# Row tiles 6, 4 and half of 5 loaded ahead of the last weight slices, and the third row tile of each later triple loaded first, in a matmul-tanh-multiply kernel

## The chip, the cores and the metric

The kernel runs on one core of a Trainium2 chip. The metric is the device time of one execution in microseconds: the median of the runs, beside the one execution that the hardware profiler took apart. The engines are TensorE (PE, with its weight loads as PEld), VectorE (DVE), ScalarE (ACT), GpSimd (POOL) and SyncE (SP). Each takes its own instructions strictly in order; DMAs are issued from the queues of SP, ACT and POOL.

## What is computed

```python
batch, m, k, n = 16, 512, 1024, 768
y1 = np.matmul(x, w1)          # x: 16 x 512 x 1024, w1 and w2: 1024 x 768, all float32
y2 = np.matmul(x, w2)
return (np.tanh(y1) * y2).astype(np.float32)
```

## The kernel before

The 8192 rows of x are 64 row tiles of 128 rows. A matmul multiplies a transposed 128 x 128 block of x (the weights that TensorE holds) by a 128 x 512 piece of w, all in float16. The 2 x 768 output columns make three blocks of 512: `a` is the first 512 columns of w1, `b` the first 512 of w2, and `g` the last 256 of both. K = 1024 falls into two halves of four 128-row slices each, so a weight slice has a name such as `b5`: block b, slice 5.

**Two ways to compute a row tile.** The first four row tiles (0 to 3, HEAD = 4) go the plain way: eight matmuls for each block (`mm`, line 421), first a, then g, then b; row 3's b part is kept for the very end. The other 60 go in 20 triples of three row tiles. A triple would take 18 products of (128 x 512) by (512 x 512), and a bilinear scheme needs only 15: p0 to p14 in C_OPS, each of them four matmuls (`product`, line 444). The operands are numbered by bits. For x, bit 2r + h is row tile r of the triple (r = 0, 1, 2), K-half h, so 16 and 32 are the two halves of the third row tile. For w, bit 3h + c is half h of block c in the order a, b, g. Other numbers are sums: S15 is the x operand 15 (`x_sum`, line 412, on DVE), B24 the w operand 24 (`w_sum`, line 403, on DVE, in two or four parts). Products accumulate in PSUM banks; between them `c_add` (line 454, DVE) and `c_copy` (line 448, ACT) move partial sums from chain to chain, so some products wait for a bank that one of these has seeded: p9 for add312, which adds p6's result to a copy. `c_tanh` (457, ACT) and `c_mul` (462, DVE) finish the outputs.

In the first triple the products come in the order 7 10 1 6 12 9 11 14 8 (FIRST_ORDER), in the later ones as in PE_ORDER, starting with p7. p7 reads operand 16 and p10 operand 32, the third row tile alone; p1 reads S3 and B24, p6 reads S15, which is S11 minus operand 4; S3 is made of row tile 0's two halves, S11 also of the second row tile's second half, S15 also of its first half. In the first triple row tiles 4, 5 and 6 are r = 0, 1 and 2.

**How x and w arrive.** x for row tiles 0 to 3 and the slices a4 to a7 and all of g come by SP's queue in float32 (a0 to a3 by ACT's) and are cast on DVE and ACT. The b slices (`load_w`, line 350) and all row tiles from 4 on (`load_x`, line 353) come by POOL's queue, which casts to float16 on the way. A `gate` instruction on POOL (line 484) holds that queue until slice g0 is cast. Then POOL issues the eight b slices in the order b0 b4 b1 b5 b2 b6 b3 b7 and after them row tiles 6, 4, 5, 7, 8, 9. From row tile 10 on each load is held (`hold_loads`, line 481) until an earlier row tile has been transposed.

**Transposes.** Row tiles 0 to 6 are transposed by TensorE (`transpose_pe`, line 371, four 128 x 128 blocks for each half) and copied out of PSUM (`evacuate`, by `copy`, line 357), for row tiles 4 to 6 by ACT. Row tiles from 7 on are transposed by a DMA on SP's queue (`transpose`, line 378). The float16 rows lie in eight buffers (xh), taken in turn by row tile, the transposed ones in twelve (xT).

**What sets the order.** All instructions are issued in an order that `Planner` works out when the kernel is built. Each operation has a cost per engine, needs, a due time, and for early loads a time at which it is taken to land (`lands`, summed from the constants in `size`, LAG and 1.25 for a whole row). The planner writes each engine's list in the order of its start times; on the chip only these lists and the semaphores remain. LANDING holds the assumed delay of a few transposes. So a change of the loads also moves instructions on TensorE, ACT and DVE.

Of the kernel before, what the change touches and what calls it, by code (L numbers as in the profile page):

```python
# [74 lines left out]
class Planner:  # L75
# [151 lines left out]
def kernel(  # L227
# [7 lines left out]
    nc = tc.nc  # L235
    P = 128
    B, M, K = x.shape
# [3 lines left out]
    MT = B * M // P  # L241
    F = 512
    G = N - F
    HEAD = 4
    TRIPLES = (MT - HEAD) // 3
    BY_PE = HEAD + 3
    FP32 = ((0, 0), (1, 0))
    LOW, HIGH = 512.0, 1024.0
    XT_BUFS, XH_BUFS, S_BUFS, O_BUFS, C_BUFS = 12, 8, 2, 9, 2
    WARM = 512, 512, 512, 512, 512, 512, 512  # L250
    FILL = 512, 512, 256
    AHEAD, FREE = 4, 3
    LANDING = {HEAD + 6: 5.8, HEAD + 7: 4.1, HEAD + 8: 3.9}
    S_AHEAD, HALVED = 4.0, 4
    LATER = {mt: 66.0 + 13.0 * mt for mt in range(HEAD - 1)}
    bf16, f16, f32, i32 = mybir.dt.bfloat16, mybir.dt.float16, mybir.dt.float32, mybir.dt.int32
# [1 line left out]
    xf = x.flatten_outer_dims().rearrange("(mt p) k -> mt p k", p=P)  # L258
# [14 lines left out]
    held = once.tile([P, 1], f32, name="held")  # L273
# [20 lines left out]
    xh_bufs = [once.tile([P, K], f16, name=f"xh{j}") for j in range(XH_BUFS)]  # L294

    def xh_place(mt):
        return (mt - HEAD) % XH_BUFS

    def xh_before(mt):
        return next((m for m in range(mt - 1, 1, -1) if xh_place(m) == xh_place(mt)), None)  # L300

    pin = tc.keep_in_program_order
    engine = {"dve": nc.vector, "act": nc.scalar, "pool": nc.gpsimd, "sp": nc.sync}
    plan = Planner(8)
    op = plan.op
# [5 lines left out]
    slices = [("a", k) for k in range(KO)] + [(s, k) for s in "gb" for k in (0, 4, 1, 5, 2, 6, 3, 7)]  # L311
# [5 lines left out]
    def w_cols(s, k):  # L317
        return wh[:, k, BLOCK[s]:BLOCK[s] + F]

    def xh(mt):  # L320
        return xh_bufs[xh_place(mt)]
# [4 lines left out]
    def half(h):  # L326
        return slice(h * KH * P, (h + 1) * KH * P)
# [21 lines left out]
        else:  # L349
            pin(nc.gpsimd.dma_start(w_cols(s, k), wr[1][:, k, :F]))  # L350

    def load_x(e, mt):
        pin(nc.gpsimd.dma_start(xh(mt), xf[mt]))  # L353

    def copy(e, dst, src):
        if e == "act":
# [123 lines left out]
    def hold_loads(e, mt):  # L480
        pin(nc.gpsimd.tensor_copy(held, xt(mt)[:, 0, :1]))  # L481

    def gate(e, s, k):
        pin(nc.gpsimd.tensor_copy(held, w_cols(s, k)[:, :1]))

    MM = 0.2158
    SLOT = KH * MM
# [17 lines left out]
    XX = 1.4  # L505
    LAG_FROM, LAG = 21.5, 1.2
    on_sp = "x00 x10 x20 x30 x01 x11 a4 a5 x21 a6 x31 a7".split() + [f"g{k}{t}" for k in range(KH) for t in range(2)]
    late = [f"b{k}" for s, k in slices if s == "b"]
    rows_in = (HEAD + 2, HEAD, HEAD + 1)
    GATE = ("g", 0)  # L510
    in_order = on_sp[4:] + late + [f"x{mt}" for mt in rows_in]
    size = {"x": 0.68, "a": 0.68, "g": 0.75, "b": 0.63}
    lands = dict(zip("x00 a0 x10 a1 x20 a2 x30 a3".split(), (4.31, 4.47, 6.13, 6.53, 7.7, 8.17, 9.05, 9.44)))
    now = 9.2
    for n in in_order:
        now += 1.25 if n in in_order[-3:] else size[n[0]]
        lands[n] = now + (LAG if now > LAG_FROM else 0.0)

    for k in range(4):
# [1 line left out]
    for n, what in enumerate(on_sp):  # L521
        before = [f"L{on_sp[n - 1]}"] if n else []
        if what[0] == "x":
            op(f"L{what}", {"sp": 0.05}, 0.1 * n - 100, [], load_first, int(what[1]), int(what[2]), issued=before, lands=lands[what])
        else:
            s, k = what[0], int(what[1])
            j = slices.index((s, k))
            old = [slices[i - SLOTS] for i in range(j, j + 1 + (s == "g")) if i >= SLOTS]
            op(f"L{what}", {"sp": 0.05}, 0.1 * n - 100, [], load_w, s, k, int(what[2]) if s == "g" else None, issued=before,
               behind=[f"c{a}{b}" for a, b in old], lands=lands[what])  # L530
    op("gate", {"pool": 0.1}, 0.0, ["c%s%d" % GATE], gate, *GATE)
    for n, what in enumerate(late):
        op(f"c{what}", {"pool": 0.58}, 0.1 * n, [], load_w, "b", int(what[1]), issued=[f"c{late[n - 1]}" if n else "gate"], lands=lands[what])
    for n, mt in enumerate(rows_in):
        op(f"L{mt}", {"pool": 0.58}, 1 + 0.1 * n, [], load_x, mt, issued=[f"L{rows_in[n - 1]}" if n else f"c{late[-1]}"],
           behind=[f"cx{m}{h}" for m in range(2, HEAD) for h in range(2) if xh_place(m) == xh_place(mt)], lands=lands[f"x{mt}"])

    landed = {}
    for s, k in slices:
# [5 lines left out]
    for t in range(2):  # L545
        for k in range(KO):
            late = START + 32 + 8 * (t * KO + k)
            op(f"aw{t}{k}", {"act": 0.81}, late + 6, [f"cg{k}", f"c{'ab'[t]}{k}"], abs_w, t, k, hold=late)

    def by_pe(mt, h, due, load):  # L550
        fp32 = (mt, h) in FP32
        op(f"PT{mt}{h}", {"pe": 0.44 if fp32 else 0.24}, due, [load], transpose_pe, mt, h, ("T", mt, h), chains=[("T", mt, h)])
        op(f"e{mt}{h}", {"dve": 0.6 if fp32 else 0.45, "act": 0.5} if mt < HEAD else {"act": 0.5}, due + 0.4, [f"PT{mt}{h}"], evacuate, mt, h, ("T", mt, h),
           chains=[("T", mt, h)])
# [3 lines left out]
    for mt in range(HEAD):  # L558
# [2 lines left out]
                op(f"cx{mt}{h}", {"dve": 0.37}, lands[f"x{mt}{h}"] - 1, [f"Lx{mt}{h}"], cast_x, mt, h)  # L561
            by_pe(mt, h, lands[f"x{mt}{h}"] - 2, f"Lx{mt}{h}" if (mt, h) in FP32 else f"cx{mt}{h}")
        op(f"D{mt}", {"act": 1.05}, START + 8, [f"Lx{mt}0", f"Lx{mt}1"], abs_x, mt, hold=11 + 4 * mt)
    for mt in rows_in:
        for h in range(2):
            by_pe(mt, h, lands[f"x{mt}"] - 2, f"L{mt}")

    def made(mt):
        return [f"e{mt}0", f"e{mt}1"] if mt < BY_PE else [f"T{mt}"]
# [1 line left out]
    xt_readers = {mt: [] for mt in range(MT)}  # L571
# [12 lines left out]
    def reuse_out(mt):  # L584
        return [f"st{mt - O_BUFS}"] if mt >= HEAD + O_BUFS else []
# [16 lines left out]
    for n, s in enumerate("agb"):  # L602
        for mt in range(HEAD):
            if (s, mt) == ("b", HEAD - 1):
                continue
            due, behind = (lambda n: landed[slices["agb".index(s) * KO + n]] + 0.8 + 0.02 * mt), []
            finals(mt, s, due(KO - 1) + (5.0, 3.0, 7.0)["agb".index(s)], plain(mt, s, due, behind))

    mt = HEAD - 1
    for t, after in enumerate(FILLERS):  # L610
# [4 lines left out]
        last = [f"m{mt}y{t}{k}" for k in range(KO)]  # L615
# [48 lines left out]
    def needed(i, v):  # L664
        return min([slot_of[i, o[0]] for o in C_OPS if o[1] == "p" and o[4] == v] + [needed(i, u) - 0.5 for u, a, b, _ in A_SUMS if v in (a, b)])

    for i in range(TRIPLES):
# [10 lines left out]
        for o in C_OPS:  # L678
            name, kind, needs = o[:3]
            needs = [f"{n}.{i}" for n in needs]  # L680
            chains = sorted({(i, p) for p in o[3:6] if isinstance(p, str) and p[0] == "c"})
            if kind == "p":
                needs += x_needs(i, o[4]) + w_needs(o[5])
                op(f"{name}.{i}", {"pe": SLOT}, slot_of[i, name], needs, product, i, *o[3:], chains=chains,
                   behind=[f"m{HEAD - 1}y0{KO - 1}"] if (name, i) == ("p3", TRIPLES - 1) else [])
# [12 lines left out]
            r = o[3]  # L698
            mt = HEAD + 3 * i + r
            due = soonest[i, name] + LAST  # L700
            if kind in ("t", "th"):
                lo, n = (0, F) if kind == "t" else (F, G)
                op(f"{name}.{i}", {"act": 0.5 if n == F else 0.285}, due, needs, c_tanh, i, r, o[4], lo, n, o[5],
                   behind=reuse_out(mt) + ([f"{FIRST_READER[name]}.{i}"] if i == TRIPLES - 1 and name in FIRST_READER else []), chains=chains)
# [4 lines left out]
            else:  # L709
                lo, n, at = (0, F, 0) if kind == "m" else (F, G, G)  # L710
                op(f"{name}.{i}", {"dve": 0.6 if n == F else 0.335}, due + 1, needs, c_mul, i, r, o[4], lo, n, at, chains=chains)
                outs[mt].insert(0 if kind == "m" else 1, f"{name}.{i}")
    for mt in range(MT):
        i = (mt - HEAD) // 3 if mt >= HEAD else -1
# [9 lines left out]
        late = [f"{('p0', 'p4', 'p11')[(mt - HEAD) % 3]}.{i + 1}"] if i < TRIPLES - 2 else []  # L724
# [3 lines left out]
                op(f"st{mt}{a}", {"sp": 0.4, "act": 0.4}, 2e4, part, store, mt, lo, n, xfer=0.4)  # L728
        else:
            op(f"st{mt}", {"sp": 0.05}, slot_of[max(i, 0), "p2"] + 12, outs[mt], store, mt, behind=late, xfer=1.0)  # L730
    for mt in range(BY_PE, MT):
        back = xh_before(mt)
        free = [] if back is None else ([f"PT{back}0", f"PT{back}1"] if back < BY_PE else [f"T{back}"]) + ([f"D{back}"] if back >= HEAD else [])
        before = f"L{mt - 1}" if mt > BY_PE else f"L{rows_in[-1]}"
        if mt >= BY_PE + FREE:
            op(f"H{mt}", {"pool": 0.1}, None, [f"T{max(mt - AHEAD, BY_PE)}"], hold_loads, max(mt - AHEAD, BY_PE), issued=[before])
            before = f"H{mt}"
        op(f"L{mt}", {"pool": 0.58}, None, [], load_x, mt, issued=[before], behind=free, xfer=XX)
        op(f"T{mt}", {"sp": 0.05}, None, [f"L{mt}"], transpose, mt, issued=[f"T{mt - 1}"] if mt > BY_PE else [],
           behind=xt_readers[mt - XT_BUFS] if mt >= XT_BUFS and mt - XT_BUFS != HEAD - 1 else [], xfer=1.2, latency=LANDING.get(mt, 1.0 if mt < HEAD + 6 else 3.0))  # L740
    for mt in range(HEAD, MT):
        i, r = divmod(mt - HEAD, 3)
        soon = START + 6 + 1.1 * r if i == 0 else slot_of[i, "p7"] + (2, 0, -4, -8)[min(i, 4) - 1] + 4.3 * r
        op(f"D{mt}", {"act": 1.05}, soon + 4, [f"L{mt}"], abs_x, mt, hold=soon)

    op("f1", {"dve": 0.3}, None, [], flag_1, behind=[f"D{mt}" for mt in range(MT)] + [f"aw{t}{k}" for t in range(2) for k in range(KO)])
    op("f2", {"dve": 0.2}, None, ["f1"], flag_2)
# [7 lines left out]
    soon = {"L" + n for n in on_sp[:4]} | {f"La{k}" for k in range(4)}  # L755
# [113 lines left out]
```

## Time and profile before

| | |
|---|---|
| Median of 3 runs | 297.97 us (297.73 to 298.39) |
| The profiled execution | 297.88 us, its span 296.3 us, 4677 instructions |
| PE busy | 289.6 us, 98% of the span |
| DVE busy | 257.4 us, 87% |
| ACT busy | 226.3 us, 76% |
| POOL busy | 49.2 us, 17% |
| Granted TensorE clock | 0.997 |
| Moved by DMA | 63.51 MB, mean 214 GB/s |

All times in a view count from the start of the span. A timeline row gives start, length, engine, line, operation, output and input tiles, shape and how many equal instructions were merged; in brackets the idle time of the engine before them, and what ended it. Matmuls overlap: one of 512 columns is shown for 0.379 us, but the next begins earlier, so a merged row is compared with the number of its matmuls. A stretch row (A:B) gives the length, the busy time and count of each engine that has any in it (PE, PEld, DVE, ACT, POOL in that order), the granted clock, the busy share of the DMA engines and GB/s. An issue row gives the tiles, the queue, the count, the size, and the time from issue to landing.

### The profile page before, as it was taken

What the parts mean: (1) busy time and instruction counts of PE and PEld (TensorE: products, weight loads), DVE (VectorE), ACT (ScalarE), POOL (GpSimd) and SP (SyncE); (2) the same over time, 40 slices, a digit from 0 to 9 for tenths busy, and PEclk for the clock granted to TensorE, in tenths of its full rate; (3) what the DMA queues carried; (4) which work ended last, traced back from release to release, by engine and by line L of the source; (5) the groups of instructions that cost most, each with busy time, mean ns of one, the idle gap of its engine ahead of it and who ended that gap; (6) DMA issues with size and microseconds to landing.
All of it is one profiled execution on the core that took longest, in us unless ns stands there. A gap on an engine that the chain in (4) does not pass through costs nothing. (4 is left out here: it accounts for less than half of the span.)

```text
span 296.3 us, 4677 instructions
## 1 busy us (share of the span) xinstructions
PE 289.6 (98%) x1374; PEld 131.9 (45%) x1374; DVE 257.4 (87%) x552; ACT 226.3 (76%) x453; POOL 49.2 (17%) x129
## 2 busy tenths in 40 slices
PE   7999999999999999999999999999999999999994
PEld 3344444444444444444444444444444444444442
DVE  1679899989999998888989898898989989898785
ACT  3586899699978979797797988768686776868442
POOL 0063033020213021102110120031012110000000
PEclk9999999999999999999999999999999999999998
DMA  6999999999999999999999999999999999340334
GB/s 215 388 307 204 183 160 149 229 197 237 224 253 271 215 198 252 237 144 253 233 234 162 221 191 218 195 310 223 221 235 232 261 269 298 127 162 25 136 141 164
DMA packets 84715, 63.51 MB, mean 214 GB/s; under 512 B 62800, under 2 KB 66896, under 8 KB 84688
## 3 DMA queue, kind: packets, MB, share of 16 engines
q1 hardware_dynamic: 73888, 44.84, 62.9%
q0 software_dynamic: 9792, 16.78, 37.2%
q10 hardware_dynamic: 1008, 1.57, 1.5%
q8 instruction: 11, 0.18, 0.3%
q14 instruction: 16, 0.13, 0.2%
HBM read 39.85 MB, written 25.17 MB: 219 GB/s over the span
## 5 line engine op out<-in xcount | busy, mean ns | idle before, releaser
L444 PE MATMUL bank<-b,early_x 128*128 128x512 f16 x640 | 148.3, 379 | 0.1
L444 PEld LDWEIGHTS <-early_x 128*128 128x128 f16 x800 | 78.1, 98 | 95.0 <-issue 0.7
L454 DVE TENSOR_TENSOR bank<-bank,arena 128x512 f32<-128x512 f32 x100 | 69.6, 697 | 14.4 <-ACT arena L448 8.8
L448 ACT ACTIVATE arena<-bank 128x512 f32<-128x512 f32 x100 | 59.4, 596 | 28.7 <-PE bank L444 28.5
L462 DVE TENSOR_TENSOR o<-o,bank 128x256 f32<-128x256 f32 (+1 forms) x132 | 64.3, 512 | 6.1 <-ACT o L457 5.4
L381 ACT ACTIVATE junk<-xh 128x1024 f16<-128x1024 f16 x60 | 63.3, 1054 | 0.2
L444 PEld LDWEIGHTS <-xT 128*128 128x128 f16 x400 | 39.0, 98 | 46.6 <-issue 0.3
L444 PE MATMUL bank<-b,xT 128*128 128x512 f16 x240 | 58.3, 379 | 0.0
L457 ACT ACTIVATE o<-bank 128x256 f32<-128x256 f32 (+1 forms) x80 | 34.5, 436 | 16.0 <-DVE bank L454 11.7
L444 PE MATMUL bank<-wh,xT 128*128 128x512 f16 x160 | 41.1, 379 | 0.0
L444 PE MATMUL bank<-wh,early_x 128*128 128x512 f16 x160 | 40.9, 379 | 0.0
L481 POOL CAST held<-xT 128x1 f32<-128x1 f16 x54 | 12.3, 227 | 159.4 <-DMA xT<-xh 159.3
L353 POOL DMA_DIRECT2D xh<-in_x_dram x60 | 31.9, 532 | 17.2 <-issue 7.7
L412 DVE TENSOR_TENSOR early_x<-early_x,xT 128x512 f16<-128x512 f16 x80 | 33.2, 419 | 0.5
L448 ACT ACTIVATE bank<-bank 128x512 f32<-128x512 f32 x40 | 21.5, 574 | 7.3 <-DVE bank L454 6.2
L457 ACT ACTIVATE o<-arena 128x512 f32<-128x512 f32 x40 | 25.1, 628 | 1.2 <-DVE arena L454 1.2
L421 PE MATMUL bank<-wh,xT 128*128 128x512 f16 x72 | 18.5, 379 | 0.5 <-DVE wh L359 0.3
L412 DVE TENSOR_TENSOR early_x<-xT,xT 128x512 f16<-128x512 f16 x40 | 16.8, 419 | 0.0
L412 DVE TENSOR_TENSOR early_x<-xT,early_x 128x512 f16<-128x512 f16 x40 | 16.8, 419 | 0.0
L454 DVE TENSOR_TENSOR bank<-arena,bank 128x512 f32<-128x512 f32 x20 | 13.9, 695 | 2.4 <-ACT o L457 0.9
L454 DVE TENSOR_TENSOR arena<-bank,arena 128x512 f32<-128x512 f32 x20 | 13.7, 683 | 0.2
L454 DVE TENSOR_TENSOR arena<-arena,bank 128x512 f32<-128x512 f32 x20 | 13.6, 681 | 0.0
(47 smaller groups left out, 134.7 us busy)
## 6 DMA issues: line engine op xcount, KB each, us to landing
out_dram<-o SPq DMA_DIRECT2D x58, 384.0 KB, 5.3
xh<-in_x_dram POOLq DMA_DIRECT2D x60, 256.0 KB, 6.8
arena<-in_w_dram SPq DMA_DIRECT2D x12, 256.0 KB, 5.6
early_x<-in_x_dram SPq DMA_DIRECT2D x8, 256.0 KB, 5.0
arena<-in_w_dram ACTq DMA_DIRECT2D x4, 256.0 KB, 5.9
wh<-in_w_dram POOLq DMA_DIRECT2D x8, 128.0 KB, 5.1
out_dram<-o SPq DMA_DIRECT2D x4, 256.0 KB, 6.5
xT<-xh SPq DMA_TRANSPOSE x57, 6.9
```

The source lines that it names most:

```text
L353: pin(nc.gpsimd.dma_start(xh(mt), xf[mt]))
L381: pin(nc.scalar.activation(junk[:, :src.shape[-1]], src, ACT.Abs, scale=scale, accum_out=sums[:, column:column + 1]))
L412: pin(engine[e].tensor_tensor(x_operand(i, v), x_operand(i, a), x_operand(i, b), OP[how]))
L421: pin(nc.tensor.matmul(bank(chain)[:, :rhs.shape[-1]], xt(mt)[:, k, :], rhs, start=first, stop=k == KO - 1, skip_group_check=True))
L444: pin(nc.tensor.matmul(place(i, dst), x_operand(i, a)[:, k, :], w_rhs(b, k), start=begins and k == 0, stop=k == KH - 1, skip_group_check=T ...
L448: pin(nc.scalar.activation(place(i, dst), place(i, src), ACT.Copy, scale=float(sign)))
L454: pin(nc.vector.tensor_tensor(place(i, dst), a, b, ALU.add if signs == (1, 1) else ALU.subtract))
L457: pin(nc.scalar.activation(out_tile(HEAD + 3 * i + r)[:, lo:lo + n], place(i, src)[:, :n], ACT.Tanh, scale=float(sign)))
L462: pin(nc.vector.tensor_tensor(o, o, place(i, src)[:, at:at + n], ALU.mult))
L481: pin(nc.gpsimd.tensor_copy(held, xt(mt)[:, 0, :1]))
```

## The change

POOL's opening queue becomes b0 b4 b1 b5, row tile 6, b2, row tile 4, b6 b3, the second half of row tile 5, b7, the first half of row tile 5. `load_x` takes columns, so that row tile 5 comes in two DMAs of 128 x 512, and each half's transposes wait for its own half. The gate takes its source as an argument and stays before b0. A list `rows` gives a new order of the row tiles from 4 on, (6, 4, 5), (9, 7, 8), (12, 10, 11) and so on: loads, transposes by DMA, holds and the choice of xh buffers follow `turn`, the place of a row tile in that list. The xT buffers still go by row tile. Of LANDING, the first entry is 4.4 for 5.8. What is computed, and the order of the products on TensorE, stay.

```diff
-    LANDING = {HEAD + 6: 5.8, HEAD + 7: 4.1, HEAD + 8: 3.9}
+    LANDING = {HEAD + 6: 4.4, HEAD + 7: 4.1, HEAD + 8: 3.9}
+    rows = list(range(HEAD)) + [HEAD + 3 * i + r for i in range(TRIPLES) for r in (2, 0, 1)]
+    turn = {mt: n for n, mt in enumerate(rows)}
...
     def xh_place(mt):
-        return (mt - HEAD) % XH_BUFS
+        return (turn[mt] - HEAD) % XH_BUFS
 
     def xh_before(mt):
-        return next((m for m in range(mt - 1, 1, -1) if xh_place(m) == xh_place(mt)), None)
+        return next((m for m in rows[turn[mt] - 1:1:-1] if xh_place(m) == xh_place(mt)), None)
...
-    def load_x(e, mt):
-        pin(nc.gpsimd.dma_start(xh(mt), xf[mt]))
+    def load_x(e, mt, cols=slice(0, K)):
+        pin(nc.gpsimd.dma_start(xh(mt)[:, cols], xf[mt][:, cols]))
...
-    rows_in = (HEAD + 2, HEAD, HEAD + 1)
-    GATE = ("g", 0)
-    in_order = on_sp[4:] + late + [f"x{mt}" for mt in rows_in]
+    by_pool = "b0 b4 b1 b5 x6 b2 x4 b6 b3 x51 b7 x50".split()
+    GATES = {"b0": ("cg0", w_cols("g", 0)[:, :1])}
+    arrivals = on_sp[4:] + by_pool
...
-    for mt in rows_in:
+    for mt in rows[HEAD:BY_PE]:
         for h in range(2):
-            by_pe(mt, h, lands[f"x{mt}"] - 2, f"L{mt}")
+            by_pe(mt, h, x_loads[mt, h][1] - 2 - 0.1 * h * (mt == HEAD + 1), x_loads[mt, h][0])
...
-    for mt in range(BY_PE, MT):
-        back = xh_before(mt)
+    for n, mt in list(enumerate(rows))[BY_PE:]:
+        back, last, held_by = xh_before(mt), rows[n - 1], rows[max(n - AHEAD, BY_PE)]
...
-            op(f"H{mt}", {"pool": 0.1}, None, [f"T{max(mt - AHEAD, BY_PE)}"], hold_loads, max(mt - AHEAD, BY_PE), issued=[before])
+            op(f"H{mt}", {"pool": 0.1}, None, [f"T{held_by}"], hold_loads, held_by, issued=[before])
...
-        op(f"T{mt}", {"sp": 0.05}, None, [f"L{mt}"], transpose, mt, issued=[f"T{mt - 1}"] if mt > BY_PE else [],
-           behind=xt_readers[mt - XT_BUFS] if mt >= XT_BUFS and mt - XT_BUFS != HEAD - 1 else [], xfer=1.2, latency=LANDING.get(mt, 1.0 if mt < HEAD + 6 else 3.0))
+        op(f"T{mt}", {"sp": 0.05}, None, [f"L{mt}"], transpose, mt, issued=[f"T{last}"] if n > BY_PE else [],
+           behind=xt_readers[mt - XT_BUFS] if mt >= XT_BUFS and mt - XT_BUFS != HEAD - 1 else [], xfer=1.2, latency=LANDING.get(n, 1.0 if n < HEAD + 6 else 3.0))
```

More of the change, by code (lines that the diff above doesn't have):

```diff
@@ L481, in hold_loads, with gate @@
         pin(nc.gpsimd.tensor_copy(held, xt(mt)[:, 0, :1]))
-    def gate(e, s, k):
-        pin(nc.gpsimd.tensor_copy(held, w_cols(s, k)[:, :1]))
+    def gate(e, src):
+        pin(nc.gpsimd.tensor_copy(held, src))
     MM = 0.2158
@@ L507 @@
     on_sp = "x00 x10 x20 x30 x01 x11 a4 a5 x21 a6 x31 a7".split() + [f"g{k}{t}" for k in range(KH) for t in range(2)]
-    late = [f"b{k}" for s, k in slices if s == "b"]
-    rows_in = (HEAD + 2, HEAD, HEAD + 1)
-    GATE = ("g", 0)
-    in_order = on_sp[4:] + late + [f"x{mt}" for mt in rows_in]
+    by_pool = "b0 b4 b1 b5 x6 b2 x4 b6 b3 x51 b7 x50".split()
+    GATES = {"b0": ("cg0", w_cols("g", 0)[:, :1])}
+    arrivals = on_sp[4:] + by_pool
     size = {"x": 0.68, "a": 0.68, "g": 0.75, "b": 0.63}
@@ L514 @@
     now = 9.2
-    for n in in_order:
-        now += 1.25 if n in in_order[-3:] else size[n[0]]
+    for n in arrivals:
+        now += 1.25 if n in by_pool and n[0] == "x" and len(n) == 2 else size[n[0]]
         lands[n] = now + (LAG if now > LAG_FROM else 0.0)
@@ L530 @@
                behind=[f"c{a}{b}" for a, b in old], lands=lands[what])
[L531 to L536, printed above, removed]
+    issued, x_loads = [], {}
+    for n, what in enumerate(by_pool):
+        if what in GATES:
+            after, src = GATES[what]
+            op(f"gate{what}", {"pool": 0.1}, 0.1 * n, [after], gate, src, issued=issued)
+            issued = [f"gate{what}"]
+        if what[0] == "b":
+            name = f"c{what}"
+            op(name, {"pool": 0.58}, 0.1 * n, [], load_w, "b", int(what[1]), issued=issued, lands=lands[what])
+        else:
+            mt, h = int(what[1]), what[2:]
+            free = [f"cx{m}{k}" for m in range(2, HEAD) for k in range(2) if xh_place(m) == xh_place(mt)]
+            name = f"L{mt}{'abc'[int(h)] if h else ''}"
+            op(name, {"pool": 0.58}, 0.1 * n, [], load_x, mt, half(int(h)) if h else slice(0, K), issued=issued, behind=free, lands=lands[what])
+            for k in range(2):
+                if h in ("", str(k)):
+                    x_loads[mt, k] = name, lands[what]
+        issued = [name]
+    last_early = name
     landed = {}
@@ L730 @@
             op(f"st{mt}", {"sp": 0.05}, slot_of[max(i, 0), "p2"] + 12, outs[mt], store, mt, behind=late, xfer=1.0)
-    for mt in range(BY_PE, MT):
-        back = xh_before(mt)
+    for n, mt in list(enumerate(rows))[BY_PE:]:
+        back, last, held_by = xh_before(mt), rows[n - 1], rows[max(n - AHEAD, BY_PE)]
         free = [] if back is None else ([f"PT{back}0", f"PT{back}1"] if back < BY_PE else [f"T{back}"]) + ([f"D{back}"] if back >= HEAD else [])
-        before = f"L{mt - 1}" if mt > BY_PE else f"L{rows_in[-1]}"
-        if mt >= BY_PE + FREE:
-            op(f"H{mt}", {"pool": 0.1}, None, [f"T{max(mt - AHEAD, BY_PE)}"], hold_loads, max(mt - AHEAD, BY_PE), issued=[before])
+        before = f"L{last}" if n > BY_PE else last_early
+        if n >= BY_PE + FREE:
+            op(f"H{mt}", {"pool": 0.1}, None, [f"T{held_by}"], hold_loads, held_by, issued=[before])
             before = f"H{mt}"
         op(f"L{mt}", {"pool": 0.58}, None, [], load_x, mt, issued=[before], behind=free, xfer=XX)
-        op(f"T{mt}", {"sp": 0.05}, None, [f"L{mt}"], transpose, mt, issued=[f"T{mt - 1}"] if mt > BY_PE else [],
-           behind=xt_readers[mt - XT_BUFS] if mt >= XT_BUFS and mt - XT_BUFS != HEAD - 1 else [], xfer=1.2, latency=LANDING.get(mt, 1.0 if mt < HEAD + 6 else 3.0))
+        op(f"T{mt}", {"sp": 0.05}, None, [f"L{mt}"], transpose, mt, issued=[f"T{last}"] if n > BY_PE else [],
+           behind=xt_readers[mt - XT_BUFS] if mt >= XT_BUFS and mt - XT_BUFS != HEAD - 1 else [], xfer=1.2, latency=LANDING.get(n, 1.0 if n < HEAD + 6 else 3.0))
     for mt in range(HEAD, MT):
         i, r = divmod(mt - HEAD, 3)
+        r = turn[mt] - HEAD - 3 * i
         soon = START + 6 + 1.1 * r if i == 0 else slot_of[i, "p7"] + (2, 0, -4, -8)[min(i, 4) - 1] + 4.3 * r
-        op(f"D{mt}", {"act": 1.05}, soon + 4, [f"L{mt}"], abs_x, mt, hold=soon)
+        op(f"D{mt}", {"act": 1.05}, soon + 4, sorted({x_loads[mt, h][0] for h in range(2)}) if mt < BY_PE else [f"L{mt}"], abs_x, mt, hold=soon)
     op("f1", {"dve": 0.3}, None, [], flag_1, behind=[f"D{mt}" for mt in range(MT)] + [f"aw{t}{k}" for t in range(2) for k in range(KO)])
```

## The prediction

> **What bounds the kernel now.** I read the page first, then the busy time by stretches, then the timeline of each engine around the change.
>
> ```profile
> span 296.3 us, 4677 instructions
> L444 PE MATMUL bank<-b,early_x 128*128 128x512 f16 x640 | 148.3, 379 | 0.1
> ```
> ```profile
> 36.00:284.00 248.00, 248.00 (x1150) 112.29 (x1149) 1.00 1.05 209
> ```
> From 36 to 284 us the matmuls of line 444 cover all of 248.00 us: 248.00/1150 = 0.2157 us from one start to the next, at a granted clock of 1.00. TensorE is the bound there and has no hole that a load could fill. A change of loads gains only where TensorE still waits, so I look for a row that is longer than its matmuls need.
>
> ```profile
> 24.09 4.91 PE L421 MATMUL bank<-wh,xT 128*128 128x512 f16 x22
> 28.84 0.61 PE L371 MATMUL bank<-ident_h,xh 128*128 128x128 f16 x8
> 29.29 0.59 PE L421 MATMUL bank<-wh,xT 128*128 128x512 f16 x2
> 32.34 4.92 PE L444 MATMUL bank<-b,early_x 128*128 128x512 f16 x20
> ```
> n matmuls need (n-1) x 0.2157 + 0.379 us. For 22 that is 4.91, as the row has it: nothing lost. For 20 it is 4.48, and the row has 4.92: **0.44 us lost**, all that this stage has to give. The weight loads say where:
>
> ```profile
> 33.49 1.62 PEld L444 LDWEIGHTS <-early_x 128*128 128x128 f16 x9 [0.62 <-DVE early_x L412]
> 35.38 2.71 PEld L444 LDWEIGHTS <-early_x 128*128 128x128 f16 x13 [0.26 <-issue]
> ```
> p1 begins at 32.34 and needs 4 x 0.2157 = 0.86, so p6 could begin at 33.20; it begins at 33.50, when VectorE's sum S15 is there: 0.30 lost. The other 0.44 - 0.30 = 0.14 falls before p9 at 35.38. Now the chain behind S15:
>
> ```profile
> 29.26 3.26 ACT L357 COPY xT<-bank 128x512 f16<-128x512 f16 x6 [2.37 <-PE bank L371]
> ```
> ```profile
> 32.15 1.29 DVE L412 TENSOR_TENSOR early_x<-early_x,xT 128x512 f16<-128x512 f16 x3
> 32.56 0.43 DVE L412 TENSOR_TENSOR early_x<-early_x,xT 128x512 f16<-128x512 f16 x1
> 34.63 0.69 DVE L454 TENSOR_TENSOR bank<-bank,arena 128x512 f32<-128x512 f32 x1
> ```
> The last of six copies of transposed rows (row 5, second half) ends at 29.26 + 3.26 = 32.52. S11 starts on it at 32.56; S15 is the third of the 1.29 us row and ends at 32.15 + 1.29 = 33.44; p6 follows at 33.50. What ends last is row 5. The 0.14 has another cause: p9 accumulates onto the seed add312, which starts after p6's last matmul and ends at 34.63 + 0.69 = 35.32. Only p12 stands between p6 and p9.
>
> **The change, part by part.**
>
> *The loads.*
>
> ```profile
> L350 POOL DMA_DIRECT2D wh<-in_w_dram x8: 537/568/669, 17.5 to 21.3; - x8
> DMA to landing us min/median/max: 3.9/5.1/5.5
> ```
> ```profile
> 21.86 0.60 POOL L353 DMA_DIRECT2D xh<-in_x_dram  x1
> 22.42 0.56 POOL L353 DMA_DIRECT2D xh<-in_x_dram  x1
> 24.03 0.54 POOL L353 DMA_DIRECT2D xh<-in_x_dram  x1 [1.05 <-DMA wh<-in_w_dram]
> ```
> ```profile
> xh<-in_x_dram POOLq DMA_DIRECT2D x1, 256.0 KB, 6.2
> ...
> xh<-in_x_dram POOLq DMA_DIRECT2D x1, 256.0 KB, 6.9
> ...
> xh<-in_x_dram POOLq DMA_DIRECT2D x1, 256.0 KB, 6.6
> ```
> ```profile
> 22.00:24.00 2.00, 2.00 (x11) 0.91 (x10) 1.93 (x6) 1.95 (x6) 0.98 (x2) 1.00 1.22 193
> 28.00:30.00 2.00, 2.00 (x21) 1.29 (x20) 2.00 (x5) 0.74 (x2) 0.00 (x0) 1.00 1.12 210
> ```
> Before, row 6 lands at 21.86 + 6.2 = 28.1, row 4 at 22.42 + 6.9 = 29.3, row 5 at 24.03 + 6.6 = 30.6. A b slice writes 131 KB, at 193 to 210 GB/s 0.62 to 0.68 us; I take 0.65. A whole row takes 1.25. In the new order b0 b4 b1 b5 x6 b2 x4 b6 b3 x5(second half) b7 x5(first half) row 6 has four slices fewer ahead: 28.1 - 4 x 0.65 = 25.5. From there on: b2 26.1, x4 27.4, b6 28.0, b3 28.7, x5's second half 29.3, b7 30.0, its first half 30.6, as row 5 before. The one extra DMA costs GpSimd 0.54 us, which lies in its idle 1.05 us. I read the 1.05, before the eleventh load of the queue, as a wait for the landing of the third; the new eleventh, b7, would then be issued at 24.0 and the half row at 24.6, five us ahead of their turn.
>
> *TensorE's queue.* By the instruction order the ten matmuls from 24.09 on stay in front; then come row 6's transposes at 24.09 + 10 x 0.2157 = 26.25 (row there at 25.5), b2 at 27.1 (26.1), p7 at 27.8, row 4's transposes at 28.6 (27.4), b6 at 29.1 (28.0), p10 at 29.7, x5's second half at 30.6 (29.3), b3 at 30.8 (28.7), x5's first half at 31.2 (30.6), p1 at 31.7, b7 at 32.5 (30.0), p6. Eight transposes cost 0.45 (28.84 to the next row at 29.29), as before. Every arrival has 0.6 us or more in hand, so moving work costs nothing if the queue keeps its rate. The same work stands ahead of p6, so its unhindered start stays at 33.20.
>
> *ScalarE.*
>
> ```profile
> 26.71 0.19 ACT L381 ACTIVATION_READ_ACCUMULATOR junk<-early_x 128x1 f32 x1
> ```
> It is free at 26.90, and a copy takes 3.26/6 = 0.54 and begins 0.42 after its transposes (28.84 to 29.26). Row 6's two copies end at 27.4 and 28.0, p7 wanting the first at 27.8; row 4's at 29.6 and 30.1; x5's second half at 31.5, its first at 31.23 + 0.42 + 0.54 = 32.2.
>
> *VectorE.*
>
> ```profile
> 25.07 1.29 DVE L403 TENSOR_TENSOR b<-wh 128x1024 f16<-128x1024 f16 x2
> 26.28 0.69 DVE L403 TENSOR_TENSOR b<-wh,b 128x1024 f16<-128x1024 f16 x1
> ```
> A weight sum costs (26.28 - 25.07)/2 = 0.60. New order: eight of them from 25.07, ending at 29.9; S3 at 30.17 on row 4's copy; S34 30.5; the second part of B24 30.85, needing b7 (30.0); S35 31.45; S11 31.8 (copy at 31.5); one weight sum; S15 at 32.7 (copy at 32.2), 0.43 long: 33.15. With the 0.06 that p6 took before, 33.21 against 33.20. **The 0.30 goes.** S15 is now paced by VectorE's own queue, with nothing in hand. The 0.14 stays, since p6, p12, p9 and the seed keep their order.
>
> *Third row first, in later triples.*
>
> ```profile
> 31.89 17.37 SPq L378 DMA_TRANSPOSE xT<-xh  x7
> 33.39 1.26 SPq L378 DMA_TRANSPOSE xT<-xh  x1
> 34.76 1.46 SPq L378 DMA_TRANSPOSE xT<-xh  x1
> ...
> 45.68 2.18 SPq L378 DMA_TRANSPOSE xT<-xh  x1
> ```
> ```profile
> xT<-xh SPq DMA_TRANSPOSE x1, 4.4
> ...
> xT<-xh SPq DMA_TRANSPOSE x1, 3.7
> ...
> xT<-xh SPq DMA_TRANSPOSE x1, 3.4
> ...
> xT<-xh SPq DMA_TRANSPOSE x1, 4.1
> ```
> ```profile
> 49.61 0.42 DVE L412 TENSOR_TENSOR early_x<-early_x,xT 128x512 f16<-128x512 f16 x1
> ```
> The number of loads and transposes on GpSimd's and SyncE's queues stays; a triple's first row is now second, its second third. Rows 7 to 9 land at 36.3, 37.1 and 38.2 whatever they are called. p7 of that triple, due about 38.5, uses the third row, which now comes first. VectorE reaches the sum on the first row at about 37.2, as five other sums now precede it, and the one on the second row at 38.1: at most 0.1 of waiting. A triple on, the third landing is 45.68 + 4.1 = 49.8 and VectorE's sum that takes it stood at 49.61: a wait of 0.2, with p6 of that triple due at 54 (18 products of 0.863 after 38.5). Bounds: below, no gain, since TensorE has no hole there; above, that 0.2 passed on whole. I take nothing, the nearest row being the gapless 248.00.
>
> **Sum.** The profiled execution took 297.88 us, its span 296.3, so 1.6 lies around it; the median of the runs is 297.97. 297.88 - 0.30 = **297.6**, 0.1% under the median.
>
> **A rule against the change.** The Trainium skill (DMA: Bandwidth & Descriptors, Anatomy of one DMA — SWDGE (gpsimd) path) gives each DMA from GpSimd a fixed 2.0 us beside its bytes. By it, taken one after another, the extra half-row would land at about 32.6 (an estimate from that page) and the time be about 299.0. The trace here speaks against adding them up, since eight such loads land within 5.4 us.
>
> **Rivals.**
>
> *A, the forecast:* 297.6, own range 297.3 to 298.0 for the 0.2 of a late sum and the scatter of the runs (297.73 to 298.39).
>
> *B, both stalls go:* 297.88 - 0.44 = 297.4. For it: the 0.14 would shrink if add312 found VectorE free sooner. Against it: the seed starts on p6's end.
>
> *C, no gain, 297.9:* S15 still ends 0.3 late, since nothing is in hand on VectorE: a row-4 copy later by that much does it.
>
> *D, slower:* row 6's transposes now stand at TensorE's head from 26.25, 2.6 us earlier than before, and everything queues behind them. Eight slices landed from 17.5 + 3.9 = 21.4 to 21.3 + 5.5 = 26.8, 5.4 us where 7 x 0.65 = 4.55 would do: the queue paused some 0.85 once. Two more such pauses ahead of row 6 bring it at 27.2, a wait of 0.95: 297.6 + 0.95 = 298.5. It decides from about 27.1 on, where the 0.30 and 0.2% are used up.
>
> *E, start-up of a load not hidden:* a lone slice lands 3.9 us after its issue, some 3.25 more than its transfer. Paid once serially, x5's first half would come at 33.9, its transposes 2.7 late: 300.3. Against it, the 5.4 us for eight slices.
>
> *F, the 0.2 of a late row passed on in several early triples:* about 298.4.
>
> **How the numbers follow.** Chances: A 0.55, B 0.15, C 0.09, D 0.15, E 0.03, F 0.03. About 0.2%, 0.6 us, is what a measurement can tell from no change. Faster by more needs under 297.37: 0.08 of A and 0.09 of B, 0.17. Slower by more: D, E and F, 0.21. Within: 0.62. The range 297.1 to 298.6 leaves out E, the upper part of D and little else, some 0.12.
>
> **What would show it.** Right: the matmul row around p1 to p8 without the 0.62 wait on L412, the wait before p9 still 0.14, row 6's transposes near 26.25 with no idle before them, 248 us without gaps. Wrong: TensorE idle before line 371's transposes between 26 and 31 us (D, E); S15 still waited for (C); waits of line 412 on transposes followed by TensorE gaps after 36 us (F).

## The result, and the profile after

| | before | after |
|---|---|---|
| Median (runs side by side) | 297.86 us (22 runs, 297.64 to 304.7) | **299.61 us** (22 runs, 297.55 to 302.58) |
| Ratio to before | | **1.0044**, 95% interval 1.0028 to 1.0060 |
| The profiled execution | 297.88 us, span 296.3 | 298.34 us, span 296.7 |

The kernel became slower, by about 0.4%, and its runs spread over several us. Ratios and their intervals, here and below, leave out executions over 1.5% above the fastest of their kernel, so they can differ from the quotient of the medians, which are over all runs. Most lines of the kernel after stand two lines lower: 412 is now 414, 444 is 446, 454 is 456, 462 is 464.

**The gain came as predicted.** TensorE's timeline of the kernel after, around p1 to p9 (4 matmuls of p1, 3 with b7 and then 16 of p6, p12, p9 and p11), and its weight loads:

```profile
26.09 0.61 PE L373 MATMUL bank<-ident_h,xh 128*128 128x128 f16 x8
...
31.53 1.03 PE L446 MATMUL bank<-b,early_x 128*128 128x512 f16 x4
32.40 0.81 PE L423 MATMUL bank<-wh,xT 128*128 128x512 f16 x3
33.04 3.76 PE L446 MATMUL bank<-b,early_x 128*128 128x512 f16 x16
```
```profile
33.03 1.62 PEld L446 LDWEIGHTS <-early_x 128*128 128x128 f16 x9 [0.32 <-DVE early_x L414]
34.91 1.17 PEld L446 LDWEIGHTS <-early_x 128*128 128x128 f16 x6 [0.26 <-issue]
```

p6 starts at 33.04 = 32.40 + 3 x 0.2157: its 0.30 is gone. The 16 matmuls need 15 x 0.2157 + 0.379 = 3.61 and take 3.76, so the 0.14 before p9 stays. Row 6's transposes stand at 26.09, with no idle before them.

**The loss comes later.** The stretch that was gapless before, and TensorE's timeline behind p7 of triple 1:

```profile
36.00:284.00 248.00, 247.41 (x1147) 111.87 (x1146) 222.34 (x480) 198.10 (x400) 41.15 (x108) 1.00 1.02 210
```
```profile
38.39 1.03 PE L446 MATMUL bank<-wh,xT 128*128 128x512 f16 x4
39.25 1.03 PE L446 MATMUL bank<-b,xT 128*128 128x512 f16 x4
40.85 1.02 PE L446 MATMUL bank<-wh,early_x 128*128 128x512 f16 x4 [0.57 <-DVE bank L456]
```

p7 of triple 1 is followed by p0 and p13 of triple 0 (the marks 0+ and 13+ in PE_ORDER). p13, due at 39.25 + 0.86 = 40.11, begins at 40.85: **0.74 lost**. It waits for add128 of triple 0 on VectorE (line 456). The expectations call this place, by its position, p13 of triple 1. VectorE's timeline there, first before, then after:

```profile
38.49 0.42 DVE L412 TENSOR_TENSOR early_x<-xT,early_x 128x512 f16<-128x512 f16 x1
38.83 0.42 DVE L412 TENSOR_TENSOR early_x<-early_x,xT 128x512 f16<-128x512 f16 x1
39.17 0.69 DVE L454 TENSOR_TENSOR bank<-bank,arena 128x512 f32<-128x512 f32 x1
```
```profile
37.70 0.69 DVE L405 TENSOR_TENSOR b<-b,b 128x1024 f16<-128x1024 f16 x1
39.30 0.88 DVE L414 TENSOR_TENSOR early_x<-early_x,xT 128x512 f16<-128x512 f16 x2 [0.92 <-DMA xT<-xh]
40.10 0.69 DVE L456 TENSOR_TENSOR bank<-bank,arena 128x512 f32<-128x512 f32 x1
```

add128 ended at 39.17 + 0.69 = 39.86 and now ends at 40.79. TensorE's timeline of before shows what slack it had: p7 at 38.85, and p13 at 40.58.

```profile
38.85 1.03 PE L444 MATMUL bank<-wh,xT 128*128 128x512 f16 x4
39.71 1.03 PE L444 MATMUL bank<-b,xT 128*128 128x512 f16 x4
40.58 1.03 PE L444 MATMUL bank<-wh,early_x 128*128 128x512 f16 x4
```

Nothing of add128 itself changed. It stands in VectorE's queue behind S11 and S15 of triple 1, and these read the triple's second and first row, which are now the third and second to be transposed. The transposes, on SyncE's queue, after:

```profile
33.48 1.91 SPq L380 DMA_TRANSPOSE xT<-xh  x1
```
```profile
35.49 1.25 SPq L380 DMA_TRANSPOSE xT<-xh  x1
```
```profile
xT<-xh SPq DMA_TRANSPOSE x1, 3.7
```

The row of 3.7 is the third's time from issue to landing. The third is issued at 35.49, behind the second, and lands at 39.2. Before it was 34.76 + 3.4 = 38.2. So two things add up: S11 and S15 need the third transpose where S15 of before needed only the second (37.1), and that third one is itself a microsecond later. The sums of the waits, of VectorE before and of all engines after:

```profile
DVE early_x L412 <- DMA xT<-xh: 0.6, 1, 0.6
```
```profile
DVE early_x L414 <- DMA xT<-xh: 2.8, 4, 1.3
...
PE bank L446 <- DVE bank L456: 0.6, 1, 0.6
```

One wait of 0.6 has become four with 2.8 in all. The profiled execution closes: 297.88 - 0.30 (p6) + 0.74 (p13) + 0.18 (before p7 of triple 4, behind a wait of 1.28 of VectorE on a transpose) = 298.50, against 298.34. But it lies 1.3 us under the median, so this cannot be all.

### The profile page after: what moved, and what is told of

Its sections match the earlier page's. It is cut to its first block, busy times and chain, and to the rows that moved or that the text cites. A ratio compares the mean times of both kernels' runs of the same rounds, so it can differ in the third digit from the quotient of the medians.

```text
span 296.7 us, 4675 instructions
## 1 busy us (share of the span) xinstructions
PE 289.8 (98%) x1374; PEld 131.7 (44%) x1374; DVE 255.5 (86%) x552; ACT 226.4 (76%) x453; POOL 50.3 (17%) x130
## 5 line engine op out<-in xcount | busy, mean ns | idle before, releaser
L450 ACT ACTIVATE arena<-bank 128x512 f32<-128x512 f32 x100 | 58.8, 596 | 16.6 <-PE bank L446 16.2
```

Source lines behind the costliest of these rows:

```text
L450: pin(nc.scalar.activation(place(i, dst), place(i, src), ACT.Copy, scale=float(sign)))
```

## The experiments

Theories, as the expectations name them. **V**: VectorE takes its work in order; the new row order makes sums wait for transposes that come one place later, and what seeds or frees a bank stands behind them. **L**: the early loads carry the loss, through the DMA queues. Two came up on the way. **W**: the planner remakes VectorE's and ScalarE's lists for all 20 triples, and these new lists cost. **T**: the last fetch of TensorE's instructions holds up the last stores.

All runs are in one table. "Idle" is TensorE's, with product and triple (p7/2 is p7 of triple 2), in the profiled execution; the last column is the time of the last 128 KB store from issue to landing. A dash under "profiled us" stands for an execution that the ratio leaves out (e1 305.93, e2 308.41, a3 304.87, t1 303.0); of these four the store is read, the idle time is not.

| kernel | median us | ratio, 95% interval | profiled us | idle in us | store |
|---|---|---|---|---|---|
| before | 297.86 | | 297.88 | p6/0 0.30 | 2.2 |
| after | 299.61 | 1.0044 (1.0028–1.0060) | 298.34 | p13/0 0.74, p7/4 0.18 | 2.2 |
| a1, a2: after, one execution each | 299.36, 299.02 | | the same | a1: p13/0 0.63; a2: p7/2 0.37, p7/3 0.43, p7/4 0.73 | 3.7, 2.3 |
| a3, a4: after | 299.87, 299.98 | 1.0061 (1.0040–1.0083), 1.0066 (1.0045–1.0087) | –, 300.39 | a4: p13/0 0.68 | 2.3, 4.2 |
| e1, e1b: loads only | 298.48, 298.45 | 1.0007 (0.9975–1.0039), 1.0024 (0.9999–1.0049) | –, 298.44 | e1b: p7/1 0.86, p7/4 0.35 | 2.3, 2.2 |
| e2, e2b: rows only | 299.05, 299.28 | 1.0007 (0.9974–1.0040), 1.0004 (0.9980–1.0028) | –, 298.79 | e2b: p6/0 0.30, p13/0 0.14, p7/2 0.18, p7/4 0.66 | 2.3, 2.3 |
| f1 | 298.37 | 1.0020 (0.9995–1.0046) | 298.20 | p7/2 0.70 | 2.2 |
| f2 | 298.61 | 1.0027 (1.0011–1.0043) | 299.63 | p7/3 0.98, 0.57 at 164, 0.24 at 169 | 2.6 |
| g1, g1b | 300.15, 299.17 | 1.0080 (1.0061–1.0098), 1.0032 (1.0012–1.0053) | 297.76, 299.48 | p7/2 0.47; 0.19 | 2.2, 3.7 |
| h2 | 300.97 | 1.0085 (1.0058–1.0111) | 301.06 | p6/0 0.30, p7/2 1.79 | 3.7 |
| h3 | 298.21 | 1.0003 (0.9971–1.0035) | 299.25 | p7/2 0.41 | 3.7 |
| t0: before, fetch moved | 297.97 | 1.0014 (0.9993–1.0034) | 298.05 | p6/0 0.30, p7/2 0.13 | 2.3 |
| t1: after, fetch moved | 299.09 | 1.0042 (1.0024–1.0060) | – | – | 2.3 |
| t2: h3, fetch moved | 298.06 | 1.0007 (0.9989–1.0025) | 298.37 | p7/3 0.37 | 2.8 |

### The parts alone, and the whole again

e1 and e1b keep the early loads and give later triples their rows in their own order (and LANDING back); e2 and e2b keep the old loads (and lose an offset of 0.1 us in the planner's time for row tile 5).

```diff
-    rows = list(range(HEAD)) + [HEAD + 3 * i + r for i in range(TRIPLES) for r in (2, 0, 1)]
+    rows = list(range(HEAD)) + [HEAD + 3 * i + r for i in range(TRIPLES) for r in ((2, 0, 1) if i == 0 else (0, 1, 2))]
```
```diff
-    by_pool = "b0 b4 b1 b5 x6 b2 x4 b6 b3 x51 b7 x50".split()
+    by_pool = "b0 b4 b1 b5 b2 b6 b3 b7 x6 x4 x5".split()
```

> The early load order alone; rows of the later triples in their old order 0, 1, 2. Theory V (the new row order makes VectorE's in-order queue wait for a late third transpose, and a product behind it): the wait on S15 before p6 stays gone, no VectorE wait of 0.9 on a transpose near 38 us, time 297.5 to 297.8 with a spread under 0.6 us. Rival L (the early loads push the row tiles 7 to 9 and their transposes back): 299 to 300.5 with a spread of several us, as the whole change has.

> The new row order alone; loads before the first triple in their old order. Theory V: p6 waits 0.3 as before, and VectorE waits for the third transpose near 38 us with TensorE idle some 0.7 us or more after it: 299 to 301, scattered. Rival L: within 0.2% of the kernel before, 297.6 to 298.3.

> The whole change once more, for a profile of another execution. Theory V: the excess over 297.6 equals TensorE's idle time behind VectorE's waits on transposes of row tiles in the first later triples (near 40 us, and again near 52 or 78 us in the longer executions). Rival L: the excess stands before 36 us or in late loads of row tiles 7 to 9.

> The same kernel a second time: the place of the idle time should stay the same and only its length change if one wait carries the scatter (V); if the idle time moves from place to place the transposes at large are late.

> The early loads alone, row order 7, 8, 9. If the third transpose lands near 39 us here too, p7 of that triple waits for it directly: 0.6 to 0.9 us idle at 38 us on TensorE and a median of 298.0 to 298.5. Theory V says that this wait is the same late transpose seen from TensorE; rival L says that this is the whole loss of the change.

> The row order alone with the old loads. Theory V: slower than before by 0.2 to 1.5 us, idle time on TensorE behind VectorE near 40, 51 and 77 us. Rival L: as the kernel before within 0.2%, with no new idle time after 36 us.

> The whole change, beside the kernels below on one chip. Theory V (VectorE's queue, in order, stands still for the third transpose of row tiles 9, 7, 8 because S11 and S15 now need it, and add128 behind them is late for p13): 298.5 to 300, scattered, TensorE idle 0.6 to 0.8 near 40 us. Rival L (early loads alone carry the loss, the row order none): the same time, so this run only sets the level.

Every kernel with early loads lost the wait before p6, and every one without kept its 0.30. Neither part alone is shown slower than before by its interval, though the medians of both lie above before's. So these runs give the loss to neither part. For the rows alone they say little: the intervals of e2 and e2b rest on 14 of 25 executions, since the other eleven took over 302 us, as 7 of 59 of the kernel before did beside them. What made those eleven long stays open. With the loads only, TensorE's timeline of e1b shows where their gain goes:

```profile
37.40 1.03 PE L446 MATMUL bank<-b,early_x 128*128 128x512 f16 x4
39.12 1.04 PE L446 MATMUL bank<-wh,xT 128*128 128x512 f16 x4 [0.69 <-DMA xT<-xh]
```

p7 of triple 1, due at 38.26, needs the third row, which is then the last to be transposed: 0.86 idle against 0.30 gained. In the whole change that row is transposed first and p7 does not wait; the wait has moved to VectorE.

### VectorE's order in the first later triples

f1 changes one assumed landing, so that the planner puts add128 and mh2 ahead of S11 and S15 of triple 1. These four places in VectorE's list are all that differs from the change in any engine's list. f2 does the same for triple 2 as well. LANDING counts by the place in `rows`, so HEAD + 5 is the third transpose of triple 1, that of its second row; two of the expectations call it the second.

```diff
-    LANDING = {HEAD + 6: 4.4, HEAD + 7: 4.1, HEAD + 8: 3.9}
+    LANDING = {HEAD + 5: 1.9, HEAD + 6: 4.4, HEAD + 7: 4.1, HEAD + 8: 3.9}
```
```diff
+    LANDING = {HEAD + 5: 1.9, HEAD + 6: 5.0, HEAD + 7: 5.2, HEAD + 8: 5.2}
```

> The whole change with one planner constant altered: the third transpose of the first later triple is assumed 0.9 us later, which moves S11 and S15 of that triple behind add128 and one multiply in VectorE's order and leaves loads, transposes and TensorE's order alone. Theory V: the idle time before p13 near 40 us goes (0.7 to under 0.1), and the kernel is 0.5 to 0.8 us faster than the whole change, unless waits in the next two triples remain, which then show as idle time before p7 near 51, 64 and 77 us. Rival L: no change against the whole change, as the loads are the same.

> The whole change, with LANDING set to 1.9, 5.0, 5.2, 5.2 for the second transpose of triple 1 and the three of triple 2: only VectorE's order is to change, add128 and mh2 ahead of S11 and S15 of triple 1, and mh1, add4, m1x, m1y ahead of the sums of triple 2 that need its second and third transposes. Theory V (VectorE's in-order queue waits for a later transpose, and what frees or seeds a bank stands behind it): no idle of TensorE over 0.2 us before p13 of triple 1 or p7 of triple 2, ratio to before 0.999 to 1.001 (about 297.6 to 298.0), with what is left at p7 of triples 3 and 4, whose order is untouched. Theory L (the early loads themselves carry the loss, through a late third transpose): the order of VectorE does not matter, ratio 1.002 to 1.005.

VectorE's timeline of f1, in triple 1 and in triple 2, and TensorE's in triple 2:

```profile
38.19 0.68 DVE L456 TENSOR_TENSOR bank<-bank,arena 128x512 f32<-128x512 f32 x1
38.79 0.41 DVE L464 TENSOR_TENSOR o<-o,bank 128x256 f32<-128x256 f32 x1
39.21 0.89 DVE L414 TENSOR_TENSOR early_x<-early_x,xT 128x512 f16<-128x512 f16 x2
```
```profile
50.24 0.42 DVE L414 TENSOR_TENSOR early_x<-xT 128x512 f16<-128x512 f16 x1 [0.85 <-DMA xT<-xh]
50.58 0.69 DVE L456 TENSOR_TENSOR bank<-arena,bank 128x512 f32<-128x512 f32 x1
```
```profile
49.66 1.89 PE L446 MATMUL bank<-b,early_x 128*128 128x512 f16 x8
52.08 1.02 PE L446 MATMUL bank<-wh,xT 128*128 128x512 f16 x4 [0.54 <-DVE o L464]
```

S11 starts as late as in the change, at 39.21, but add128 is past it at 38.19, and the idle before p13 is gone: V's mechanism is shown at its first place. Beside a3, on the same chip and with the same loads, f1's ratio to before is 1.0020 where a3's is 1.0061, which speaks against L as the whole cause; their two intervals overlap a little. The wait then stands at the next place: S3 of triple 2 waits 0.85 for the second transpose, and the multiplies that free p7's bank stand behind it: 0.70. f2 cleared that too, and p7 of triple 3 lost 0.98. V's number for f2 (297.6 to 298.0) was missed: 298.61.

### Third row first in two triples only

LANDING is as in f1.

```diff
-    rows = list(range(HEAD)) + [HEAD + 3 * i + r for i in range(TRIPLES) for r in (2, 0, 1)]
+    rows = list(range(HEAD)) + [HEAD + 3 * i + r for i in range(TRIPLES) for r in ((2, 0, 1) if i < 2 else (0, 1, 2))]
```

> Early loads as in the change, third row first in triples 0 and 1 alone, rows in their own order from triple 2 on; LANDING 1.9 for the second transpose of triple 1. In triple 1, p7 then has its row first (as in the whole change) and VectorE has add128 ahead of S11; from triple 2 on the order of rows, and nearly that of VectorE, is that of the kernel before. Theory V: the 0.30 before p6 gone, no idle over 0.2 us before p7 and p13 of triple 1 nor before p7 of triples 2 to 4, ratio 0.9985 to 0.9995 (about 297.5). Theory L: as with the early loads alone, ratio 1.001 to 1.004.

> The kernel of g1_two_triples once more, beside the two with lists, for a median from more runs: it had 300.15 from six, and 297.76 in the execution that was profiled. If its loss is real, the median is above 298.5 and well above that of the kernel with the same head and the lists of before (theory W); if six runs misled, about 297.6.

A plain miss for V: one execution at 297.76, the others from 299.43 up, and again 299.17 in twelve runs of g1b. The idle that V speaks of was 0.47 and 0.19. Something else cost more than a microsecond; in the profile of g1b it is the last store, 3.7 for 2.2.

### The lists of VectorE and ScalarE

Names in each engine's list are taken from lists written out. h2 is the kernel before, VectorE and ScalarE after 36 us in the order that the planner makes for e1; TensorE, SyncE and GpSimd unchanged. h3 has g1's start with f2's LANDING, and from 52 us on before's order on TensorE, VectorE and ScalarE.

```diff
+                    if e in LISTS and LISTS[e][at[e]:at[e] + 1] != [n]:
+                        continue
...
+            if e in at:
+                at[e] += 1
```

> The kernel before (its loads, its rows, its order on TensorE, SyncE and GpSimd), but VectorE and ScalarE take their work after about 36 us in the order that the planner makes for the early loads alone; nothing else differs. Theory W (the planner, replanning all 20 triples, leaves orders on VectorE and ScalarE whose waits for late transposes and late stores reach TensorE): slower and spread, 298.3 to 299.5 median, ratio 1.002 to 1.006. Theory V (only the first few triples' sums, waiting for transposes that come later, cost): as before, ratio 0.999 to 1.001, about 297.9. Theory L (the early loads themselves cost through the DMA queues): as before too, there being none.

> Early loads as in the change, third row first in triples 0 and 1 alone, VectorE's sums of triple 1 and 2 behind what frees banks (LANDING 1.9, 5.0, 5.2, 5.2), and from about 52 us on TensorE, VectorE and ScalarE take their work in the order of the kernel before, written out as lists. Theory W: 297.4 to 297.7, spread no more than before, ratio 0.9985 to 0.9995. Theory V: the same, if no idle is left before p7 of triple 2. Theory L: 298.5 or more and spread, ratio 1.002 to 1.006, since loads are as in the change.

In h2 no load, row order or product was touched, and it was slower than before by no less than the whole change: 1.0085 (1.0058 to 1.0111). GpSimd's timeline near 39 us and DMA issues between 40 and 52 us, before and then h2:

```profile
38.56 0.53 POOL L353 DMA_DIRECT2D xh<-in_x_dram  x1
```
```profile
xT<-xh SPq DMA_TRANSPOSE x4, 5.6
```
```profile
39.97 0.53 POOL L358 DMA_DIRECT2D xh<-in_x_dram  x1 [1.39 <-ACT junk L386]
```
```profile
xT<-xh SPq DMA_TRANSPOSE x4, 9.1
```

The order on ScalarE decides when an xh buffer comes free, through the |x| sums that read it (line 381, here 386): the load waits 1.39 for one. The four transposes in this stretch then took 9.1 at the median, not 5.6, and p7 of triple 2 came 1.79 late. That the later load made the transposes slow is likely and not shown. So a list alone can cost.

But this wait is not one that the changed kernel has. The load is that of row 12. In before, rows 12, 13 and 14 take the buffers of rows 4, 5 and 6, and ScalarE's list has the |x| sums of rows 4, 5, 6 in this order. e1's list has 6, 4, 5, which suits e1, where the buffers go by `turn` and row 12 takes row 6's. h2 joins e1's list to before's buffers, so row 12 waits for the sum of row 4, now the second. In e1b, with the list and the buffers that belong together, the same load does not wait:

```profile
38.68 0.53 POOL L355 DMA_DIRECT2D xh<-in_x_dram  x1
```

Nor is a rest left in h2 for other places of its lists: the profiled execution is 3.2 us longer than before's, and the 1.79 and the last store (3.7 for 2.2) make 3.3. So h2 does not show that the change loses by its new lists; W stays untested there. h3 does not settle it: its ratio of 1.0003 is under those of g1 and g1b (1.0080 and 1.0032), but its interval overlaps g1b's and does not exclude a loss of 0.35%.

### The last instruction fetch

In five of the nineteen profiles the last store lands 3.7 to 4.2 us after its issue, in the others after 2.2 to 2.8. DMA queues in the last us, in the kernel before, a1 and a4:

```profile
q14 instruction: 1, 0.01, 0.8%
...
out_dram<-o SPq DMA_DIRECT2D x1, 128.0 KB, 2.2
```
```profile
q8 instruction: 1, 0.02, 1.4%
q14 instruction: 1, 0.01, 0.7%
...
out_dram<-o SPq DMA_DIRECT2D x1, 128.0 KB, 3.7
```
```profile
q8 instruction: 1, 0.02, 2.5%
q14 instruction: 1, 0.01, 0.6%
...
out_dram<-o SPq DMA_DIRECT2D x1, 128.0 KB, 4.2
```

All five, and only they, have a q8 packet of 16 KB there, 1.3 to 2.2 us after the start of the last matmul; in the others it came 1.6 to 4.9 us before that start. q8 has 11 packets in every profile. To move it, the last of seven warming matmuls became nine small ones, in the kernels before (t0), after (t1) and h3 (t2):

```diff
-    WARM = 512, 512, 512, 512, 512, 512, 512
+    WARM = (512,) * 6 + (64,) * 9
...
-        constants(banks[n], cols)
+        constants(banks[n % 7], cols)
```

> The kernel before with the last of its seven warming matmuls (512 columns) replaced by nine of 64 columns: about the same time on TensorE, but 8 matmuls and 8 weight loads more in its instruction stream, which brings every later 16 KB piece of it to be fetched about 8 x 0.2157 = 1.7 us earlier. A control. Theory T (the last fetch of TensorE's instructions, queue q8, holds the last stores up where it comes some 2 us after the last matmul has begun): before fetches it at -3.3 us already, so ratio 0.9990 to 1.0010. Otherwise the same.

> The whole change with the same nine small warming matmuls. Theory T: the last q8 fetch moves from -2.0 or +2.1 us to about -3.7, never among the last stores; executions that were 1.4 us longer for it go, those with late sums stay: median 298.2 to 298.8 where the whole change has 299.5, ratio 1.0010 to 1.0035. Theory V or W alone (late sums and orders carry all of the loss): as the whole change beside it, ratio 1.004 to 1.008.

> The kernel of h3 (early loads, third row first in triples 0 and 1, before's lists of TensorE, VectorE and ScalarE from 52 us on) with the same nine small warming matmuls. Theory T: the upper group of h3's runs (298.85 to 299.71) goes and the lower stays: median 297.5 to 298.0, spread under 1 us, ratio 0.9990 to 1.0010. Without it: as h3, median 298.2, runs to 299.7.

> The whole change, unchanged, beside the three with more warming matmuls on the same chip: 299.4 to 300.0, ratio 1.004 to 1.008, by every theory.

Eight more matmuls moved the fetch from -3.3 to -4.9 us (t0), and from between -2.0 and +2.2 to -3.3 (t1, t2), so q8 carries TensorE's instructions; none of the three has the late store. (Three profiles would be few for that alone; that the late store goes with the fetch rests on all nineteen.) The Trainium skill (Runtime: NRT & Kernel Launch, Instruction fetch mechanics) says that an engine's instructions are refilled in blocks of 16 KiB over a DMA queue of its own, at a cost "mostly hidden". The packets' size and queue agree; that the cost is hidden does not hold here, where the last store lands 1.5 to 2.0 us later with a fetch beside it. How the fetch holds the store up, the traces don't show. The median of t1 is 0.9 us under that of the unchanged kernel beside it, and above its forecast of 298.2 to 298.8. The intervals of t1 and a4 overlap, so the runs alone do not fix the size; the profiles do, at 1.5 to 2.0 us each time. t2, the best, is 298.06, and no version beat the kernel before. But t2 has the early loads and no loss that shows, 1.0007 (0.9989 to 1.0025), so L can carry little of the change's.

## Why the prediction was wrong, point by point

**The loads: right.** Row 6 landed at 19.60 + 6.0 = 25.6 (forecast 25.5). Row 6 and the last two of the early queue, b7 and the half row behind it, in GpSimd's timeline and in its issues after:

```profile
19.60 0.56 POOL L355 DMA_DIRECT2D xh<-in_x_dram  x1
...
24.12 0.53 POOL L352 DMA_DIRECT2D wh<-in_w_dram  x1 [1.23 <-DMA wh<-in_w_dram]
24.64 0.53 POOL L355 DMA_DIRECT2D xh<-in_x_dram  x1
```
```profile
xh<-in_x_dram POOLq DMA_DIRECT2D x1, 256.0 KB, 6.0
```
```profile
wh<-in_w_dram POOLq DMA_DIRECT2D x1, 128.0 KB, 6.0
xh<-in_x_dram POOLq DMA_DIRECT2D x1, 128.0 KB, 6.1
```

The last two landed at 30.1 and 30.7, 0.6 apart. The Trainium skill's fixed 2.0 us for each DMA of this path (DMA: Bandwidth & Descriptors, Anatomy of one DMA — SWDGE (gpsimd) path), added up, gave the prediction's 32.6 for the last one, and the trace does not agree; nor did rival E happen. Nor did D: row 6's transposes have no idle before them. What failed is in the rest:

- **The 0.30: right,** in all fourteen profiles with early loads. **The 0.14: right.**
- **"Third row first, in later triples … I take nothing, the nearest row being the gapless 248.00": the step that failed.** It was rival F, given 0.03. The prediction took as fixed what the change moved: "Rows 7 to 9 land at 36.3, 37.1 and 38.2 whatever they are called" held within 0.3 for the first two in the profile after; the third landed there at 39.2 (39.0 in a1, 39.6 in a4, but 38.1 in a2 and a3). "At most 0.1 of waiting" was 0.92 in one row. And a gapless stretch of before says only that its waits stayed inside their slack: by the rows above, add128 had 40.58 - 39.86 = 0.72. Against that, add128 came 0.93 later and p7 0.46 earlier (38.39 for 38.85). The gain itself took part of the slack. And for triple 2 the prediction looked at p6, due at 54, not at p7, which needs a bank that VectorE frees behind such sums (a2 lost 0.37 there, f1 0.70).
- **Size of F:** forecast 298.4, measured 299.6. Late sums cost 0.63 to 1.53 in the four profiles of the change read here; with -0.30 that gives 298.2 to 299.1. Above that lies the last fetch, 1.5 to 2.0 in two profiles of five (a1, a4). With it the four close within 0.4 us: 298.5 for 298.34, 299.7 for 299.36 (a1), 299.1 for 299.02 (a2), 300.3 for 300.39 (a4). How often each of the two falls in the other executions is not known, so the median is not closed.
- **Left out altogether:** that the planner makes new lists for all 20 triples, and where the instruction fetch falls (T). Neither had a term, since the prediction followed only the instructions that the diff moves. The second goes with 1.5 to 2.0 us in two profiles; that the first cost anything, beyond the late sums, is not shown.
- **Open:** why the second transpose is issued over 1.7 to 1.9 us in some executions with early loads and 1.25 in others; why the fetch of the changed kernel comes later than before's, with as many matmuls (counted in the traces, TensorE's list has 2776 instructions for before's 2777, and h2's, with a fetch as late as any, 2772; whether that is the cause was not tested); how the 0.4 to 0.7% divide between V, T and perhaps W.

## What to carry to other kernels

Before an order of arrival is costed at nothing, take for each engine the operations that stand behind the first one that now waits, and compare the wait with the slack of the nearest of them, after the gain is taken off that slack. Where a planner writes the lists, a local edit is an edit of every list. A run that has only the new lists tells their cost only if they fit the buffers of the kernel that they are put into; h2's did not. A median that lies above what the profiled execution explains asks for more profiles of the same kernel, and for the landing times of its last stores.

## What the runs showed of the hardware that was not expected

- A 16 KB fetch of TensorE's instructions among the last stores goes with a last 128 KB store that lands 3.7 to 4.2 us after its issue instead of 2.2 to 2.8, in five of five profiles against none of fourteen.
- Eight warming matmuls more, costing no time that shows (t0: 1.0014, 0.9993 to 1.0034), moved that fetch 1.6 us earlier.
- A DMA transpose of the same size, on the same queue, took from 3.4 to over 9 us to land (3.4 for the third one of before, 9.1 the median of four in h2).
